# New order of a half in a gated convolution and state-space step: gates between the u tiles, convolution output kept in DRAM, phase tables from sines, planner durations reset

## The chip, the cores and the metric

The kernel runs on one core of one Trainium2 chip. The metric is device time in microseconds (us) of one execution. The kernel before takes 1961.19 us (median of three runs, 1960.9 to 1964.42).

## The reference, cut to what matters

One layer is applied to 2048 prompt tokens and to 8 single tokens that carry a state. Width 1024, state-space branch 512 wide in 32 groups of 16 channels with 64 complex states, convolution of 31 taps.

```
h    = rmsnorm(x, g_pre)
proj = h @ w_in          # c_a, c_b, c_z (1024 each), s_x, s_z (512 each), g_c, g_s (1024 each)
u    = c_a * sigmoid(c_b)
v    = silu(layernorm(causal_depthwise_conv(u))) * silu(c_z)
y_c  = v @ w_pc
ys   = gelu(ssm_branch(s_x))          # s_t = lambda * s_(t-1) + B u_t, lambda = exp((a_re + i a_im) dt)
ys   = ys * sigmoid(ys @ w_glu + b_glu) * silu(s_z)
y_s  = ys @ w_ps
o    = (sigmoid(g_c) * y_c + sigmoid(g_s) * y_s) @ w_out
x1   = x + rmsnorm(o, g_post)
e    = rmsnorm(p @ w_ple, g_ple)
y    = x1 + e * sigmoid(x1 @ w_pg + b_pg)
```

## The kernel before, in words

Channels lie on the 128 partitions, tokens along the free side. The tokens go in two halves: half 0 has 1024 prompt tokens and the 8 single ones (1032 columns in three blocks of 344), half 1 has 1024 (two blocks of 512). From `w_out` on, half 0 is worked in two parts of 516 columns, each as two blocks of 258. Every product is made in three fp32r matmuls: high part of the activations with high and low part of the weights, and low part with the high one (lines 289 to 291 of `stages`; lines 307 to 309 of `stage_pair`, where two weights share one pass). A name that ends in h or l is such a part: `hh`/`hl` of h, `yh`/`yl` of the gelu'd SSM output, `ynh`/`ynl` of the gated one, `mh`/`ml` first of the gate sum and then of x1.

A **stage** is one weight tile of 128 output channels: raw weights come by DMA on SP's queue into one of two buffers, ScalarE casts them to `whi` (line 252), GpSimd subtracts for `wlo` (line 332), one stage ahead of its use. TensorE runs the stage block by block into one of six PSUM banks, and a function given with the stage empties each bank. All engines run their instructions in the order in which the program emits them.

The order of emission comes from two sources. The list `order` (lines 218 to 234) gives the weight tiles: in half 0 the SX tiles (s_x) twice (first block, then the two others), CB and CA of each u tile, the eight GC gates, SZ, `w_glu`, then two GS gates ahead of each of the four `w_ps`, CZ, `w_pc`, `w_out`, `w_pg`. Half 1 is alike. Everything beside the stages is a task of a planner, `Background` (lines 30 to 104): a task is a generator that names an engine and a ready time, `use` adds an estimated duration (`cV`, `cS`, `cG`, lines 138 to 142) to that engine's clock, `pick` chooses VectorE or GpSimd, and `pump` emits all that should have begun by TensorE's estimated time. `drain` emits a task to its end at once, whatever the clocks say. Tasks are the norms (`mean_task`, `rstd_task`, `norm_task`), the convolution (`conv_task`: 31 multiply-adds on VectorE into an accumulator `acc` in PSUM, with some taps made by ScalarE and GpSimd, `cq` and `ca`), the state-space tables (`ssm_setup`, among them the phase tables `ph` by repeated doubling, and the transposes of `gt` by TensorE, line 610), the state-space batches (`ssm_batch`: scans between two turns by the phases), the layer norm, the x1 tiles (per tile a multiply `o<-o,prm,oacc` of line 183, an add `o<-o,xr`, a cast `mh<-o` on ScalarE, and `ml<-o,mh`) and the h tiles of the next half (`xn`, `hh`, `hl`). Activations of 128 x 1096 live in 38 SBUF units, taken and freed as the program goes; `room(n)` makes a task wait for n free ones.

Of the kernel before, what the change touches and what calls it, by code (L numbers as in the profile page):

```python
# [23 lines left out]
NUNIT = 38  # L24
UW = 1096


class Background:
# [19 lines left out]
    def pump(self, until=None, prio=1e9, only=None, pe=True):  # L48
        end = self.pe if until is None else until
        low = min(self.now, end)  # L50
        while True:
            best, first = None, 0.0
            for t in self.tasks:
                if t[0] > prio:
                    break
                e, r = t[1]
                if e == "P" and only and r > self.pe and not any(t is x for x in only):
                    continue
                if e == "P" and not pe:
                    continue  # L60
                at = max(self.clock[e], r) if e in self.clock else r + (1.2 if e == "P" else 0.0)
                if at <= end and (best is None or at < first - 0.05):
                    best, first = t, at
            if best is None:
                self.now = end
                return
            self.now = max(low, first)
            try:
                best[1] = next(best[2])
            except StopIteration:  # L70
                best[3] = True
                self.tasks.remove(best)
# [61 lines left out]
def build(nc, tc, A, O):  # L134
# [23 lines left out]
    with ExitStack() as ctx:  # L158
# [60 lines left out]
        for h in range(2):  # L219
            if h == 0:  # L220
                order += [("w_ple", j) for j in range(2)]
            for _ in range(2 if h == 0 else 1):
                order += [("w_in", SX + b) for b in range(4)]
            for c in range(8):
                order += [("w_in", CB + c), ("w_in", CA + c)]
# [56 lines left out]
        def stages(key, todo):  # L282
            wt, k = take(key)
            for i, (m, rhs, evac, c0, n) in enumerate(todo):
# [9 lines left out]
                bg.pe += 3 * k * (n / 2400.0 + 0.003)  # L294
# [3 lines left out]
        def stage_pair(keys, rhs, blocks, evacs):  # L298
# [12 lines left out]
            bg.pe += 6 * len(rhs) * sum(n / 2400.0 + 0.003 for _, n in blocks)  # L311
# [36 lines left out]
        def mean_task(acc, blocks, bias, ready, k, split):  # L348
# [11 lines left out]
            yield "P", ready  # L360
# [32 lines left out]
        def norm_task(acc, blocks, ready, split=False):  # L393

            c = slice(blocks[0][0], blocks[-1][0] + blocks[-1][1])
            (tmp, y), r = yield from mean_task(acc, blocks, epsc, ready, 2, split)
# [14 lines left out]
        ud_d = [dram.tile([P, HT + NS], F32, name=f"ud{b}") for b in range(NB)]  # L411
        yd_d = [dram.tile([P, 8, 136], F32, name=f"yd{b}") for b in range(NB)]
# [18 lines left out]
        MAGIC = 12582912.0  # L431

# [15 lines left out]
        tables = {"done": 0}  # L448

        def ssm_setup():  # L450
# [20 lines left out]
            r0 = use("V", 5.6, 3.0)  # L471
# [8 lines left out]
            r0 = use("V", 1.6, r0)  # L480
# [25 lines left out]
            r0 = use("V", 4.0, r0)  # L506
# [19 lines left out]
            r0 = use("V", 6.0, r0)  # L526
# [16 lines left out]

            yield "V", r0
            tt(k1, mag, mag)
            tt(k1, k1, k1)
            tt(rho, k1, k1)
            ph = [[k1, k2], [k3, nre]]

            def unit_length(re, im, t):  # L550

                tt(t[0], re, re)
                tt(t[1], im, im)
                tt(t[0], t[0], t[1], ALU.add)
                ts(t[0], t[0], -0.5, 1.5)
                tt(re, re, t[0])
                tt(im, im, t[0])

            v2 = [wk[:, x * 16:x * 16 + 16] for x in range(2)]
            V.tensor_copy(out=ph[0][0], in_=cs)  # L560
            V.tensor_copy(out=ph[0][1], in_=sn)
            for x in range(3):
                unit_length(*ph[0], v2)
                cmul(*ph[1], *ph[0], *ph[0], *v2)
                ph.reverse()
            r0 = use("V", 6.5, r0)
            for x in range(2):
                yield from room(3)
                pu2 = [alloc(name="ph") for _ in range(3)]
                un = [t[:, 0:1024].rearrange("p (j k) -> p j k", k=P) for t in pu2[0:2]]  # L570
                w2 = [pu2[2][:, y * 512:(y + 1) * 512].rearrange("p (j k) -> p j k", j=8) for y in range(2)]
                s2 = [t[:, 0:8] for t in v2]
                yield "V", r0
                for r in range(2):
                    V.tensor_copy(out=un[r][:, :, 0], in_=ph[0][r][:, x * 8:x * 8 + 8])
                m = 1
                while m < P:
                    unit_length(un[0][:, :, m - 1], un[1][:, :, m - 1], s2)
                    base = [u_[:, :, m - 1:m].to_broadcast([P, 8, m]) for u_ in un]
                    cmul(un[0][:, :, m:2 * m], un[1][:, :, m:2 * m], un[0][:, :, 0:m], un[1][:, :, 0:m],  # L580
                         *base, w2[0][:, :, 0:m], w2[1][:, :, 0:m])
                    m *= 2
                    r0 = use("V", 2.0 + 6 * cV(4 * m), r0)
                    yield "V", r0
                for b in range(2 * x, 2 * x + 2):
                    for r in range(2):
                        dma(out=ph_d[b][:, r * 512:(r + 1) * 512],
                            in_=pu2[r][:, (b - 2 * x) * 512:(b - 2 * x + 1) * 512], after=r0)
                free(*pu2)
            r1 = max(r0, r1)  # L590
            for b in range(NB):
# [11 lines left out]
                r1 = use("V", 6 * cV(512), r1)  # L603
                we = alloc(name="we")
                wev = we[:, 0:1024].rearrange("p (j i r s) -> p j i r s", i=2, r=2, s=64)
                for r in range(2):
                    yield "P", r1
# [7 lines left out]
                yield "P", r1  # L615
# [7 lines left out]
                free(gt)  # L623
                yield "V", r3
# [13 lines left out]
                free(kdu, we)  # L638
                cq = alloc(name="cq")
# [18 lines left out]
                tables[b] = queue["data"] + 1.0  # L658
            free(bb, bcu, cbd, pu)
# [16 lines left out]
        def ssm_batch(h, b, sx, ysb, n, ready):  # L676
# [25 lines left out]
            phu = alloc(name="sph")  # L702
            rp = dma(out=phu[:, 0:1024], in_=ph_d[b], after=tables[b])
# [8 lines left out]
            for j0 in range(0, 4, 2):  # L712
                yield "P", r
# [16 lines left out]
            r = max(r1, rp)  # L730
# [16 lines left out]
            r = use("V", 2 * cV(1024) + 2 * cV(512), r)  # L747
# [6 lines left out]
            r = use("V", 8 * cV(256), r)  # L754
# [3 lines left out]
            r = use("V", 2 * cV(1024) + 2 * cV(512) + 0.2, r)  # L758
# [9 lines left out]
            for j0 in range(0, 4, 2):  # L768
                yield "P", r
# [51 lines left out]
        def conv_task(h, us, vs, seen):  # L821
            for c in range(NT):
                while us[c] is None:
# [10 lines left out]
                use("V", 0.4)  # L834
# [10 lines left out]
                use("V", 1.33)  # L845
                while left["lo"] <= left["hi"]:
# [6 lines left out]
                    r = use("V", 1.33)  # L853
# [34 lines left out]
        def sample_conv_task(seen):  # L888

            w = lambda c, k: cw[:, c, k:k + 1]  # L890
            for c in range(NT):
# [12 lines left out]
                use("V", 1.0, r)  # L904
# [23 lines left out]
        def embed(wait):  # L928

            for j in range(2):  # L930
                def ev_of(h, j=j):
# [3 lines left out]
                    def ev(m, o, c0, nn):  # L935
# [3 lines left out]
                        if c0 == 344:  # L939
                            V.tensor_copy(out=ts_[m][:, c0:c0 + nn], in_=o)  # L940
                            fore("V", cV(nn) + 0.06)
# [24 lines left out]
        def rms_task(todo):  # L966

            for nm, h in todo:
# [25 lines left out]
                r = yield from norm_task(acc, BLOCKS[h], ra, True)  # L994
# [85 lines left out]
        def half(h, hT, finish):  # L1080
# [16 lines left out]
            for k, part in enumerate(PARTS[h] if h == 0 else [[0, 1]]):  # L1097
                if finish:
                    finish(k)
                def ev_of(b):  # L1100
# [21 lines left out]
            us, vs = [None] * NT, [None] * NT  # L1122
            seen = [0, 0]
            conv = bg.add(conv_task(h, us, vs, seen), 10)
            samp = bg.add(sample_conv_task(seen), 9) if h == 0 else None
            for c in range(NT):
                sg = unit("sg")
                stage(("w_in", CB + c), hT, blocks, act_to(sg, AF.Sigmoid))
                u = unit("u")

                def ev_a(m, o, c0, nn, sg=sg, u=u):
                    tt(u[:, PAD + c0:PAD + c0 + nn], o, sg[:, c0:c0 + nn])
                    fore("V", cV(nn) + 0.06)

                stage(("w_in", CA + c), hT, blocks, ev_a)
                free(sg)
                us[c] = (u, bg.clock["V"] + 0.3)
# [3 lines left out]

            for c in range(NT):
                gc = unit("gc")
                stage(("w_in", GC + c), hT, blocks, act_to(gc, AF.Sigmoid))
                dma(out=gc_d[h][c * P:(c + 1) * P, 0:n], in_=gc[:, 0:n], after=bg.clock["S"] + 0.3)
                free(gc)
# [5 lines left out]
            def gelu_task(b):  # L1152
                yield "S", ready[b]
                zs[b] = alloc(name="z")
# [52 lines left out]
            def ysn_task(b):  # L1207
                yield "S", ready[b]
                ysn[b] = hilo("yn")
# [9 lines left out]
            cz, vT = [None] * NT, [None] * NT  # L1219
            zr = [0.0] * NT  # L1220

            lnt = {}

            def ln_sub(c, mean, acc, r):
                yield "V", r
                v = vs[c][0][:, PAD:PAD + n]
                r = ew("V", v, v, mean[:, full], ALU.subtract, n, r)
                if c:
                    yield from room(1)
                q = alloc(name="sq") if c else acc  # L1230
                yield "S", r
                S.activation(out=q[:, full], in_=v, func=AF.Square)
# [354 lines left out]
```

## Time and profile before

| | |
|---|---|
| profiled execution | 1960.78 us, span 1959.0 us |
| runs | 1960.9, 1961.19, 1964.42 us |
| granted clock of TensorE, mean | 0.991 |
| busy: PE / DVE / ACT / POOL | 1915.9 / 1438.4 / 769.3 / 784.2 us |
| DMA | 243.63 MB, mean 124 GB/s |
| share of the chain that ended last: PE / DVE / issue / POOL / ACT | 84 / 4 / 3 / 2 / 2 % |

TensorE has work for 98% of the span. The page's slices show where it has not: the first two slices (0 to 98 us) and the fourth and fifth (147 to 245 us). The table of waits names what it waited for each time.

### The profile page before, as it was taken

How to read it: one execution, taken by the hardware profiler on the slowest of the kernel's cores; microseconds unless marked ns; L12 is line 12 of the kernel's file. 1: busy time of each engine (PE TensorE's matmuls, PEld its weight loads, DVE VectorE, ACT ScalarE, POOL GpSimd, SP SyncE). 2: the span in 40 equal slices, each digit the busy share in tenths (PEclk: the TensorE clock that was granted, in tenths of full speed). 3: DMA queues.
4: the chain of work that ended last, by engine and by line, in shares of the span. 5: the costliest groups of instructions: out<-in, count | busy, mean ns of one | idle time of the engine just before them, and what ended most of it. 6: DMA issues, size and time to landing. Idle time of an engine off the chain costs nothing.

```text
span 1959.0 us, 27432 instructions
## 1 busy us (share of the span) xinstructions
PE 1915.9 (98%) x10772; PEld 1723.5 (88%) x10772; DVE 1438.4 (73%) x1703; ACT 769.3 (39%) x1301; POOL 784.2 (40%) x573
## 2 busy tenths in 40 slices
PE   8897999999999999999999999999999999999998
PEld 7897999999999999999997888888788888888876
DVE  6889997899899876446674579888499843341786
ACT  7424211228311364255533223455731353223542
POOL 1437523315422233234452222786743223224554
PEclk9898999999999999999999999999999999999999
DMA  8461334542122215334564563222112311432455
GB/s 316 152 209 56 106 133 142 181 141 71 57 89 80 99 43 194 120 95 144 193 207 162 183 204 119 65 65 97 66 43 76 99 65 44 161 108 86 140 193 172
DMA packets 103290, 243.63 MB, mean 124 GB/s; under 512 B 11752, under 2 KB 41576, under 8 KB 103144
## 3 DMA queue, kind: packets, MB, share of 16 engines
q1 hardware_dynamic: 102840, 241.68, 37.0%
q8 instruction: 84, 1.38, 0.3%
q14 instruction: 46, 0.38, 0.1%
q10 hardware_dynamic: 320, 0.20, 0.0%
HBM read 188.17 MB, written 54.62 MB: 124 GB/s over the span
## 4 chain that ended last, share of the span: by engine, by line
PE 84%; DVE 4%; issue 3%; POOL 2%; ACT 2%; DMA 1%; SPq 0%; ACTq 0%; POOLq 0%; DVEq 0%
PE bank L289 27%; PE bank L291 26%; PE bank L290 26%; PE bank L775 2%; POOL ca L332 1%; PE bank L778 1%; PE bank L720 1%; DVE sgp L332 1%; POOL wlo L332 1%; DVE o L183 1%; DMA raw<-in_w 1%; DVE spar L183 0%; DVE o L332 0%; PE bank L620 0%; DMA xn<-in_xT 0%
## 5 line engine op out<-in xcount | busy, mean ns | idle before, releaser
L332 POOL TENSOR_TENSOR wlo<-raw,whi 128x512 fp32r<-128x512 f32 x386 | 565.7, 1484 | 1072.2 <-ACT whi L252 1056.8
L289 PE MATMUL bank<-hh,whi 128*128 128x344 f32 (+1 forms) x1888 | 666.1, 353 | 0.9 <-ACT whi L252 0.9
L290 PE MATMUL bank<-hl,whi 128*128 128x344 f32 (+1 forms) x1888 | 661.4, 350 | 5.3 <-DVE hl L332 5.3
L291 PE MATMUL bank<-hh,wlo 128*128 128x344 f32 (+1 forms) x1888 | 659.8, 349 | 1.5 <-POOL wlo L332 1.5
L183 DVE SCALAR_TENSOR_TENSOR acc<-u,prm,acc 128x1024 f32<-128x1024 f32 x412 | 530.5, 1288 | 11.2
L289 PEld LDWEIGHTS bank<-hh,whi 128*128 128x128 f32 x1888 | 356.6, 189 | 37.5 <-ACT whi L252 1.5
L290 PEld LDWEIGHTS bank<-hl,whi 128*128 128x128 f32 x1888 | 357.1, 189 | 36.8 <-DVE hl L332 5.6
L291 PEld LDWEIGHTS bank<-hh,wlo 128*128 128x128 f32 x1888 | 357.4, 189 | 34.7 <-POOL wlo L332 2.5
L252 ACT CAST whi<-raw 128x512 fp32r<-128x512 f32 x388 | 223.9, 619 | 144.0 <-PE bank L290 68.7
L289 PE MATMUL bank<-mh,whi 128*128 128x258 f32 (+1 forms) x768 | 247.0, 322 | 2.2 <-ACT mh L339 1.7
L291 PE MATMUL bank<-mh,wlo 128*128 128x258 f32 (+1 forms) x768 | 246.6, 321 | 1.7 <-POOL wlo L332 1.6
L290 PE MATMUL bank<-ml,whi 128*128 128x258 f32 (+1 forms) x768 | 246.5, 321 | 0.4 <-DVE ml L332 0.3
L291 PEld LDWEIGHTS bank<-mh,wlo 128*128 128x128 f32 x768 | 145.6, 190 | 14.3 <-POOL wlo L332 3.0
L289 PEld LDWEIGHTS bank<-mh,whi 128*128 128x128 f32 x768 | 145.4, 189 | 14.2 <-ACT mh L339 1.9
L290 PEld LDWEIGHTS bank<-ml,whi 128*128 128x128 f32 x768 | 145.5, 189 | 12.5 <-DVE ml L332 1.0
L332 POOL TENSOR_TENSOR ca<-ca,cq 128x512 f32<-128x512 f32 x104 | 132.3, 1300 | 38.9 <-ACT cq L882 35.6
L290 PE MATMUL bank<-vl,whi 128*128 128x344 f32 (+1 forms) x320 | 111.9, 350 | 0.7 <-DVE vl L332 0.7
L289 PE MATMUL bank<-vh,whi 128*128 128x344 f32 (+1 forms) x320 | 112.0, 350 | 0.0
L291 PE MATMUL bank<-vh,wlo 128*128 128x344 f32 (+1 forms) x320 | 111.9, 350 | 0.0
L882 ACT ACTIVATE cq<-u,prm 128x512 f32<-128x512 f32 x104 | 73.4, 722 | 55.1 <-POOL ca L332 46.0
L332 DVE TENSOR_TENSOR oacc<-oacc,sq 128x258 f32<-128x258 f32 (+1 forms) x42 | 29.7, 721 | 70.2 <-ACT sq L1389 69.9
L177 DVE TENSOR_TENSOR gcl<-bank,gcl 128x344 f32<-128x344 f32 (+1 forms) x40 | 23.5, 587 | 65.4 <-PE bank L291 65.3
(213 smaller groups left out, 2452.0 us busy)
## 6 DMA issues: line engine op xcount, KB each, us to landing
raw<-in_w SPq DMA_DIRECT2D x194, 512.0 KB
cq<-cq SPq DMA_DIRECT2D x12, 512.0 KB
e<-e SPq DMA_DIRECT2D x8, 516.0 KB
rt<-e SPq DMA_DIRECT2D x8, 516.0 KB
gc<-gc SPq DMA_DIRECT2D x8, 516.0 KB
m<-gs SPq DMA_DIRECT2D x8, 516.0 KB
gcl<-gc SPq DMA_DIRECT2D x8, 516.0 KB
m2l<-m SPq DMA_DIRECT2D x8, 516.0 KB
```

What stands on the lines that cost most here:

```text
L177: V.tensor_tensor(out=out, in0=a, in1=b, op=op)
L183: V.scalar_tensor_tensor(out=out, in0=a, scalar=s, in1=b, op0=op0, op1=op1)
L252: S.copy(out=hi, in_=t[:, c])
L289: T.matmul(o, hi[:, w], rh[:, c0:c0 + n], start=kt == 0, stop=False)
L290: T.matmul(o, hi[:, w], rl[:, c0:c0 + n], start=False, stop=False)
L291: T.matmul(o, lo[:, w], rh[:, c0:c0 + n], start=False, stop=kt == k - 1)
L332: (V if e == "V" else GP).tensor_tensor(out=out, in0=a, in1=b, op=op)
L720: T.matmul(pvs[rr][half_[i], jj], we[:, g * P + rr * 64:g * P + rr * 64 + 64], U[:, g, 8:8 + ne], start=True, stop=True)
L775: T.matmul(pvs[i][:, jj], TW[:, :, 2 * j + i], U[:, 2 * j + i, o0:136], start=True, stop=False)
L778: T.matmul(pvs[i][:, jj], cq[half_[i], x * 512 + j * P:x * 512 + (j + 1) * P], X[half_[i], x, j, o0:136], start=False, stop=x == 1)
L882: S.activation(out=q[:, h], in_=u[:, k + x * 512:k + x * 512 + 512], func=AF.Identity, scale=w(k))
```

## The change

1. Half 0 starts with two u tiles on block 0 (in place of SX), then the same two on blocks 1 and 2, then the four SX tiles, then the other u tiles. Two of the 16 gate stages follow each later u tile; the rest of the gates come ahead of SZ. In half 1 all eight u tiles have two gates each.
2. All gates, the GS ones too, are stored to DRAM. The GS gates are loaded again as `gs` before `w_ps`, and the four `w_ps` follow each other directly after `w_glu`.
3. The convolution's output tiles 0 to 5 may be stored to DRAM (`v_d`) and loaded again by `back_task`, added after `w_ps`.
4. The phase tables are made with Sin on ScalarE and products on GpSimd (`phases`), in place of doubling on VectorE.
5. The planner's durations are new, and a task's matmul may be marked "Q": it is laid 9 us of planned time later.

The transposes move to line 655, the helpers to lines 343, 184 and 190, and the products to lines 300 to 302 of the changed kernel. Core of the diff:

```
+                if e == "Q":
+                    e, r = "P", r + MARGIN
-        return "V" if v + n / 960.0 <= g + n / 478.0 + 0.3 else "G"
+        return "V" if v + n / 760.0 <= g + n / 440.0 + 0.4 else "G"
-    cV = lambda n: 0.08 + n / 960.0
+    cV = lambda n: 0.12 + n / 760.0
-    cS = lambda n: 0.13 + n / 1250.0
-    cG = lambda n: 0.16 + n / 478.0
+    cS = lambda n: 0.15 + n / 1100.0
+    cG = lambda n: 0.3 + n / 440.0
...
-            order += [("w_in", GC + c) for c in range(8)]
+            for c in range(0 if h else EARLY, 8):
+                order += [("w_in", CB + c), ("w_in", CA + c)] + gates[:2]
+                gates = gates[2:]
+            order += gates
             order += [("w_in", SZ + b) for b in range(4)]
             order += [("w_glu", j) for j in range(2)]
-            for j in range(4):
-                order += [("w_in", GS + 2 * j), ("w_in", GS + 2 * j + 1), ("w_ps", j)]
+            order += [("w_ps", j) for j in range(4)]
...
+            def phases(x, r):
...
+                r = ew("G", v3(a), kb, part(hi), ALU.mult, 1024, r)
+                r2 = ew("G", v3(cp), kb, part(lo), ALU.mult, 1024, r)
...
+                S.activation(out=sp, in_=a, func=AF.Sin, scale=PI)
+                S.activation(out=cp, in_=q, func=AF.Sin, scale=-PI, bias=hpi)
...
-            for x in range(2):
-                yield from room(3)
...
-                    unit_length(un[0][:, :, m - 1], un[1][:, :, m - 1], s2)
...
-                    cmul(un[0][:, :, m:2 * m], un[1][:, :, m:2 * m], un[0][:, :, 0:m], un[1][:, :, 0:m],
-                         *base, w2[0][:, :, 0:m], w2[1][:, :, 0:m])
...
+            def back_task():
+                lnt["back"] = True
+                for c in list(lnt["out"]):
+                    yield from room(6)
+                    t = alloc(name="v")
+                    vs[c] = t, dma(out=t[:, PAD:PAD + n], in_=v_d[h][c * P:(c + 1) * P, 0:n])
...
+            load_gs(0)
             for j in range(4):
-                gs = [unit("gs") for _ in range(2)]
-                for x in range(2):
-                    stage(("w_in", GS + 2 * j + x), hT, blocks, act_to(gs[x], AF.Sigmoid))
                 if j == 0:
                     bg.drain(*yt)
...
                 stt(o[:, cc], o[:, cc], vcol("g_post", c), acc[:, cc], ALU.mult, ALU.mult)
-                r = max(use("V", cV(m), r), rx)
+                r = max(use("V", 0.2 + m / 420.0, r), rx)
```

Three places show how instructions move. First, VectorE at the start, where it makes the low parts `hl` of the first half's blocks 1 and 2 (the 688 column rows). Before:

```order
L177 TENSOR_TENSOR acc_169<-acc_169,mean_339 128x688
...
L183 SCALAR_TENSOR_TENSOR xT_138<-xT_138,prm,acc_169 128x688
L183 SCALAR_TENSOR_TENSOR xT_139<-xT_139,prm,acc_169 128x688
...
L332 TENSOR_TENSOR hl_418<-xT_138,hh_417 128x688
L332 TENSOR_TENSOR hl_420<-xT_139,hh_419 128x688
```

The same place in the changed kernel, where `spar` are the 16 column parameters of the state-space branch and `u` is what empties a bank of a u tile:

```order
L184 TENSOR_TENSOR acc_173<-acc_173,mean_606 128x688
...
L184 TENSOR_TENSOR u_765<-bank,sg_687 128x344
L190 SCALAR_TENSOR_TENSOR xT_142<-xT_142,prm,acc_173 128x688
...
L190 SCALAR_TENSOR_TENSOR xT_144<-xT_144,prm,acc_173 128x688
L184 TENSOR_TENSOR u_839<-bank,sg_802 128x344
L343 TENSOR_TENSOR hl_416<-xT_142,hh_415 128x688
...
L190 SCALAR_TENSOR_TENSOR xT_147<-xT_147,prm,acc_173 128x688
...
L343 TENSOR_TENSOR hl_430<-xT_149,hh_429 128x688
```

The first `hl` tile now stands behind the emptying of the second u tile's block 0, and 14 rows of `spar`, left out here, stand ahead of it too, between the first row and the second.

Second, TensorE at the end of `w_glu` in half 0. Before, the products of `yh` are followed by two GS gates on `hh`, 144 matmuls, and only then by `ynh`:

```order
L290 MATMUL bank<-yl_4706,whi 128x344
L291 MATMUL bank<-yh_4705,wlo 128x344
L289 MATMUL bank<-hh_417,whi 128x344
L290 MATMUL bank<-hl_418,whi 128x344
...
L291 MATMUL bank<-hh_431,wlo 128x344
L289 MATMUL bank<-ynh_5183,whi 128x344
```

In the changed kernel:

```order
L300 MATMUL bank<-yh_5428,whi 128x344
L301 MATMUL bank<-yl_5429,whi 128x344
L302 MATMUL bank<-yh_5428,wlo 128x344
L300 MATMUL bank<-ynh_5914,whi 128x344
L301 MATMUL bank<-ynl_5915,whi 128x344
```

No stage is left between the two.

Third, ScalarE in part 1 of `w_out` of half 0, where `mh` are the high parts of part 0's x1 tiles and `whi` the weights of a coming stage. Before, the casts are spread over the stages:

```order
L339 CAST mh_7276<-o_8108 128x516
L339 CAST mh_7378<-o_8109 128x516
L321 COPY o_8110<-bank 128x258
L252 CAST whi<-raw 128x512 x2
...
L339 CAST mh_7489<-o_8110 128x516
...
L252 CAST whi<-raw 128x512 x2
...
L339 CAST mh_7597<-o_8111 128x516
...
L252 CAST whi<-raw 128x512 x2
```

In the changed kernel all eight stand within one stage:

```order
L263 CAST whi<-raw 128x512 x2
L350 CAST mh_7204<-o_8020 128x516
L350 CAST mh_7304<-o_8021 128x516
...
L350 CAST mh_7407<-o_8022 128x516
L350 CAST mh_7510<-o_8023 128x516
L350 CAST mh_7613<-o_8024 128x516
...
L350 CAST mh_7819<-o_8026 128x516
L350 CAST mh_7918<-o_8027 128x516
L332 COPY o_8023<-bank 128x258
L263 CAST whi<-raw 128x512 x2
```

The next cast of weights comes behind the last of them. The same lump stands in half 1.

## Rows read from the trace of the kernel before

**Rows 1.** The page, part 1: busy time of each engine, its share, instructions.

```profile
PE 1915.9 (98%) x10772; PEld 1723.5 (88%) x10772; DVE 1438.4 (73%) x1703; ACT 769.3 (39%) x1301; POOL 784.2 (40%) x573
```

**Rows 2.** TensorE's waits: what was waited for, total us, times, longest us.

```profile
PE bank L610 <- issue: 14.1, 1, 14.1
PE bank L289 <- ACT whi L252: 8.3, 3, 6.9
PE bank L290 <- DVE hl L332: 5.3, 1, 5.3
PE bank L289 <- ACT mh L339: 1.7, 1, 1.7
```

**Rows 3.** Stretches: bounds, length, busy of PE, PEld, DVE, ACT, POOL, clock, DMA.

```profile
522.40:545.00 22.60, 22.60 (x146) 22.60 (x145) 19.62 (x22) 8.61 (x14) 10.30 (x6) 1.00 0.18 53
890.00:936.00 46.00, 46.00 (x381) 45.89 (x380) 30.84 (x41) 26.38 (x60) 22.98 (x16) 1.00 0.45 149
84.50:88.00 3.50, 3.40 (x12) 3.40 (x13) 2.77 (x21) 1.73 (x4) 0.00 (x0) 0.50 0.05 20
196.00:200.00 4.00, 3.77 (x15) 3.80 (x16) 3.93 (x7) 1.21 (x2) 1.28 (x1) 0.50 0.39 137
990.00:994.00 4.00, 4.00 (x22) 4.00 (x23) 3.93 (x4) 1.79 (x5) 2.98 (x2) 0.59 0.17 63
```

**Rows 4.** Timeline, 186 to 198 us, VectorE and TensorE: start, us, instruction, idle before.

```profile
188.84 2.02 DVE L177 TENSOR_TENSOR ph<-ph 128x512 f32<-128x512 f32 x3
195.44 0.69 DVE L177 TENSOR_TENSOR gt<-gw 128x512 f32<-128x512 f32 x1
196.23 1.09 PE L610 MATMUL bank<-ident,gt 128*128 128x128 f32 x4 [14.06 <-issue]
```

**Rows 5.** Timeline, 50 to 85 us, VectorE and TensorE, and a group of VectorE's.

```profile
50.86 2.63 DVE L183 SCALAR_TENSOR_TENSOR xT<-xT,prm,acc 128x688 f32<-128x688 f32 x3
83.68 0.87 DVE L332 TENSOR_TENSOR hl<-xT,hh 128x688 fp32r<-128x688 f32 x1
84.60 0.65 PE L290 MATMUL bank<-hl,whi 128*128 128x344 f32 x1 [5.33 <-DVE hl L332]
L332 DVE TENSOR_TENSOR hl<-xT,hh 128x688 fp32r<-128x688 f32 x7 | 5.9, 871 | 4.0 <-ACT hh L339 4.0
```

**Rows 6.** Timeline of ScalarE and VectorE after `w_glu` of half 0.

```profile
522.63 0.55 ACT L1192 ACTIVATE sgl<-bank,prm 128x344 f32<-128x344 f32 x1 [1.36 <-PE bank L291]
523.08 3.91 ACT L339 CAST ynh<-z 128x1032 fp32r<-128x1032 f32 x4
524.16 4.67 DVE L332 TENSOR_TENSOR ynl<-z,ynh 128x1032 fp32r<-128x1032 f32 x4 [0.43 <-ACT ynh L339]
L332 DVE TENSOR_TENSOR ynl<-z,ynh 128x1024 fp32r<-128x1024 f32 x4 | 4.6, 1217 | 0.0
```

**Rows 7.** Timeline of VectorE, 901 to 964 us, and groups of x1 instructions.

```profile
901.32 0.69 DVE L177 TENSOR_TENSOR oacc<-oacc,mean 128x516 f32<-128x516 f32 x1
931.94 0.70 DVE L332 TENSOR_TENSOR ml<-o,mh 128x516 fp32r<-128x516 f32 x1 [0.35 <-ACT mh L339]
955.60 0.74 DVE L183 SCALAR_TENSOR_TENSOR o<-o,prm,oacc 128x516 f32<-128x516 f32 x1
962.83 3.48 DVE L183 SCALAR_TENSOR_TENSOR o<-o,prm,oacc 128x516 f32<-128x516 f32 x2
L183 DVE SCALAR_TENSOR_TENSOR o<-o,prm,oacc 128x516 f32<-128x516 f32 x16 | 21.9, 1396 | 0.0
L332 DVE TENSOR_TENSOR o<-o,xr 128x516 f32<-128x516 f32 x16 | 15.0, 959 | 0.0
L332 DVE TENSOR_TENSOR ml<-o,mh 128x516 fp32r<-128x516 f32 x16 | 11.8, 762 | 1.4 <-ACT mh L339 1.3
```

**Rows 8.** TensorE's waits from 1896 to 1920 us (`w_pg` of half 1).

```profile
PE bank L291 <- POOL wlo L332: 1.6, 2, 1.1
PE bank L289 <- ACT whi L252: 0.5, 1, 0.5
```

More of the change, by code (lines that the diff above doesn't have):

```diff
@@ L24 @@
 NUNIT = 38
+NSPILL = 6
+MARGIN = 9.0
+EARLY = 2
 UW = 1096
@@ L310, in stage_pair @@
             w_ahead(wstate["use"], 0)
-            bg.pe += 6 * len(rhs) * sum(n / 2400.0 + 0.003 for _, n in blocks)
+            bg.pe += 6 * len(rhs) * sum(cPr(n) for _, n in blocks)
             bg.pump(pe=False)
@@ L411, in build @@
         ud_d = [dram.tile([P, HT + NS], F32, name=f"ud{b}") for b in range(NB)]
+        v_d = [dram.tile([D, HT + NS], F32, name=f"v{h}") for h in range(2)]
         yd_d = [dram.tile([P, 8, 136], F32, name=f"yd{b}") for b in range(NB)]
@@ L446, in exp_dve @@
             tt(out, q, ki.bitcast(F32))
-        tables = {"done": 0}
+        tables = {"done": 0, "phases": 0}
         def ssm_setup():
@@ L507, in ssm_setup, with phase_task @@
+            def phase_task(r):
+                for x in range(2):
+                    yield from phases(x, r)
+            bg.add(phase_task(r0), 6.1)
             yield "V", r0
@@ L658, in ssm_setup @@
                 tables[b] = queue["data"] + 1.0
+            while tables["phases"] < NB:
+                yield None, bg.now + 0.5
             free(bb, bcu, cbd, pu)
@@ L729, in ssm_batch @@
             free(we)
-            r = max(r1, rp)
+            while tables["phases"] < b + 1:
+                yield None, bg.now + 1.0
+            yield from room(3)
+            phu = alloc(name="sph")
+            r = max(r1, dma(out=phu[:, 0:1024], in_=ph_d[b], after=tables["ph", b // 2]))
+            yield from room(2)
             tmp, tm2 = alloc(name="stmp"), alloc(name="stmq")
@@ L1099, in half @@
+            ln = bg.add(ln_task(), 4)
+            conv = bg.add(conv_task(h, us, vs, seen), 10)
+            samp = bg.add(sample_conv_task(seen), 9) if h == 0 else None
+            if h == 0:
+                for k, part in enumerate(PARTS[h]):
                     finish(k)
+                    for c in range(EARLY):
+                        u_tile(c, [blocks[i] for i in part])
+            for part in [list(range(len(blocks)))]:
                 def ev_of(b):
@@ L1121, in half, with gate @@
                 bg.add(rms_task([("e", 1)]), 7)
[L1122 to L1137, printed above, removed]
+            def gate(i):
+                t = unit("gc")
+                stage(("w_in", (GC, GS)[i // 8] + i % 8), hT, blocks, act_to(t, AF.Sigmoid))
+                dma(out=(gc_d, m2_d)[i // 8][h][i % 8 * P:(i % 8 + 1) * P, 0:n], in_=t[:, 0:n],
+                    after=bg.clock["S"] + 0.3)
+                free(t)
+            gate_at = 0
+            for c in range(0 if h else EARLY, NT):
+                u_tile(c, blocks)
+                for _ in range(2):
+                    gate(gate_at)
+                    gate_at += 1
             if h == 0:
                 dma(out=O["conv_old"], in_=A["cache"][:, 1:, :])
[L1142 to L1146, printed above, removed]
+            while gate_at < 16:
+                gate(gate_at)
+                gate_at += 1
             bg.drain(*tasks, wait=False)
```

358 lines of the change are left out of this document (215 added, 143 removed).

## The prediction

> **What bounds the kernel now.** I read the page first: TensorE is busy for 1915.9 of 1959.0 us, VectorE for 1438.4 [rows 1]. The change leaves TensorE's matmuls as they are, 10,120 rows of the program before and after. So less work elsewhere (VectorE 1705 instructions to 1488, GpSimd 578 to 655, ScalarE 1303 to 1380) gives nothing by itself, and the sum is one of TensorE's stalls: which go, which come. The second view is TensorE's waits [rows 2]. One is large, 14.1 us before the first transposes (L610). Of the 8.3 us for `whi`, 6.9 is the first weight load, which stays. Third come the stretches: 144 matmuls of 344 columns take 22.6 us, 0.157 us each, and between 890 and 936 us, where x1 is made beside `w_out`, TensorE never waits although VectorE is busy for 30.8 us of 46 [rows 3].
>
> The stretches show a second price. After the 5.3 us wait and after the 14.1 us one the granted clock is 0.50 [rows 3], which is 1.2 of 2.4 GHz, and it is 0.59 over the 4 us after the 1.7 us wait for `mh`. In the 3.5 us after the first, 12 matmuls are done where 3.5 / 0.157 = 22 would have been, so 10 x 0.157 = 1.6 us are lost, and the rise ends a few matmuls later. I count 1.7 us for every stall of some 2 us or more, added or removed.
>
> **The start.** Before, the 688 column `xT` begin right after the norm, at 50.86, and the last `hl`, behind the parameters, starts at 83.68; TensorE waits 5.33 us for it, until 84.60 [rows 5]. Four stages of block 0 are done by then, and 7/8 of the next one, 3.3 of 24 x 0.157 = 3.77 us, so block 0 ends at 84.6 - 5.3 - 3.5 = 75.8. In the changed order (two u tiles in place of the SX, the same four stages) all eight `hl` and five `xT` stand behind the eviction of the second u tile's block 0, which waits for that end. With 0.5 for the eviction, 8 x 0.87 and 5 x 0.88 (2.63 for three [rows 5]) the last `hl` ends at 87.7; TensorE needs it at 79.3. The wait is 8.4 in place of 5.3, and longer beside `wlo`. I take +4; the ends are -5 (it goes, GpSimd or gaps taking the rows) and +7. The clock fell there before, too.
>
> **What goes.** The transposes wait for `gt`. The timeline shows why: VectorE does the doubling (`ph`, still 2.02 us at 188.84) ahead of the `gt` products, and the transposes start 0.1 us behind the end of the first `gt`, 195.44 + 0.69 [rows 4]. In the changed kernel VectorE doubles nothing, and behind the last `hl` stand parameters, four evictions and seven taps, then `gt`: by the durations of such rows in the trace some 35 us, 40 with small operations at the slow 1.2 us that they have beside `wlo`, so about 123 to 128. TensorE has 14 more blocks of 3.77 us ahead of the transposes from 75.8 (eight of the u tiles, six of SX), and the stall: 75.8 + 8.4 + 1.7 + 52.8 = 139. I take the stall as gone: -14.1 - 1.7 = -15.8. The ends are that, and 0, where as much as before stands ahead of `gt`.
>
> At the second part's `w_pg` in half 0 the wait for `mh` was 1.7 us [rows 2]. The x1 rows now come with 25 us of VectorE rows up to the last `ml`, before with 34, as the gate products stand behind them: -1.7 - 1.7 = -3.4, between 0 and that.
>
> **`w_glu` to `w_ps`.** Two GS stages of 11.3 us covered the making of `yn` [rows 3]. They are gone, the stage behind `w_glu` reads `ynh` and `ynl` at once. `w_glu`'s last bank is read at 522.63, some 0.2 us after its end; four `ynh` casts run from 523.08 to 526.99 and the fourth `ynl` ends at 528.83 [rows 6], 6.4 us behind 522.4. A stage with four pairs needs the fourth low part after 3 x 0.47 + 0.16 = 1.6 us. The stall is 4.8 us, with the clock 6.5. In half 1 the casts and `ynl` have the same sizes (4.6 us for four `ynl` [rows 6]) and a stage of 512 columns needs the last after 2.3: 4.5, with the clock 6.2. Together +12.7. The lower bound is 6, if the first two pairs are made while `w_glu` still runs; the upper is 15, if VectorE has a tap of 1.3 us between.
>
> **x1 beside `w_out`.** Before, the tiles are spread: the first multiply follows `oacc` (which ends at 902.0) and the last `ml` ends at 932.6, 30 us and five stages of 5.8 us later, with weight casts between [rows 7]. In the changed order eight adds, eight casts `mh` and six of the eight multiplies are laid into one stage, because its eviction drains older tasks, and the next `whi` stands behind them on ScalarE. VectorE's rows behind `oacc` are 8 x (1.396 + 0.959 + 0.762) = 25 us by the means. The chain begins some 4 us before that stage, the last `mh` is out at about +20, and the `whi` behind it was due when TensorE has worked that stage and the one after, at 2 x 5.8 = 11.6: a stall of 9 us. But the same multiply takes 0.74 alone and 1.74 beside GpSimd's `wlo` [rows 7], and while `whi` is held no `wlo` runs. With 2.1 us per tile the chain is 17 us and the stall 1 to 2. I take 5 us in half 0 and, with 14.9 us of rows in one stage, 4 in half 1, each with the clock: 5 + 4 + 3.4 = +12.4. Ends 0 and 22.
>
> The Trainium skill ("SBUF — State Buffer", "SBUF: two separate sides") says that a VectorE operation with two SBUF inputs and a GpSimd operation that reads SBUF take a port pair by an exclusive lock, and that the loser waits for the whole instruction. The trace agrees for this multiply: 0.74 alone against 3.48 / 2 = 1.74 [rows 7]. By that rule the lump speeds up as soon as GpSimd has no weights to split, the two stalls fall to 1 to 2 us each, and the sum is about +8 (1969); by the means they are 9 each and it is about +25 (1986).
>
> **`w_pg` of half 1.** It waited 1.6 + 0.5 = 2.1 us for weights [rows 8]. In the changed order the norm comes two stages later and all x1 tiles in one stage, VectorE 15 us against 5.6 of TensorE. I take a stall of 5 and the clock, 6.7 - 2.1 = +4.6, between -2 and +9.
>
> **Rest.** The layer norm of half 1 is laid into three stages in place of eight (VectorE 37 us against 33 of TensorE), +1 (0 to 5). ScalarE has 31 us of rows in two stages of 23.5 us around SZ of half 0, and seven h tiles, before five, are left to the end of half 0: together +1 (0 to 8). The convolution taps, the phase work of GpSimd (eight products per two batches, 11.7 us of rows per 11.3 us stage at most) and some 29 MB more DMA lie beside TensorE; I cost them at nothing as long as VectorE and GpSimd do not fall behind by a stage. If they do, a bank is emptied late, and each late stage costs its lateness once.
>
> **Sum.** -15.8 - 3.4 + 4 + 12.7 + 12.4 + 4.6 + 1 + 1 = +16.5. The profiled execution took 1960.8 us, 0.4 below the median of the runs shown: 1977.3, against the median 1977.7. I say 1977.
>
> **Rivals.**
> Covered: VectorE, with 73 us less of rows, is ahead at each of the new places, the lumps run at the price without GpSimd and hide, and the `yn` are begun early. Then -15.8 - 3.4 + 0 + 6 + 0 - 2 + 0 + 0 = -15, 1946. For it speaks the span from 890 to 936 without a wait; against it, that the fourth `ynl` depends on the last bank of `w_glu`, whoever is ahead. 0.22.
> Balance: the lumps hide, the start and `w_ps` cost what they cost: -19.2 + 4 + 12.7 + 0 + 2 = -0.5, 1960. 0.12.
> The stall stays: `gt` is late all the same, since the parameters are more (nine small operations for the phases) and each takes 1.2 us beside GpSimd. Half of 15.8 stays, and the lumps cost 9 each in place of 5 and 4: 1977 + 8 + 9 = 1994. Against it speaks that nothing long stands ahead of `gt`. 0.14.
> My forecast, 1966 to 1988 by its own bounds, has 0.52. It ends slower, and the Covered case on the other side; the lump decides from the point where the last `mh` comes less than 11.6 us behind the stage's start.
>
> This kernel's measurement can tell 0.2% from no change, about 4 us. Faster: Covered and a bit of Balance, 0.24. Same: 0.10. Slower: the rest, 0.66. The range goes from 1944, just under Covered, to 1996, just over the third rival, and leaves about 0.15 out.
>
> **What would show it.** Right: the largest wait at the transposes is gone; TensorE waits for `hl` by 8 us or more near 78 us; waits for `ynl` of 4 to 5 us twice, each followed by a clock near 0.5; a wait for `whi` in the second part of `w_out`, in each half, after the last of eight `mh`. Wrong: no wait at `ynl`, or `w_out` without one, or a long wait in the convolution's stretch for a bank or for weights behind a held DMA.

## The result and the profile after

The changed kernel takes 2006.99 us (median of four runs, 2006.52 to 2009.29) against 1961.05 us: ratio 1.0233, 95% interval 1.0215 to 1.0251. It is slower by 46 us. The forecast was slower, 1977 us, with a range from 1944 to 1996: the sign is right, the size is not.

The page of the changed kernel, part 1, answers to [rows 1]; its matmuls are the same in number, VectorE is busy for 55 us less, ScalarE for 60 and GpSimd for 118 us more:

```profile
PE 1935.8 (97%) x10772; PEld 1732.0 (86%) x10772; DVE 1383.7 (69%) x1486; ACT 828.9 (41%) x1378; POOL 901.9 (45%) x650
```

TensorE's waits of the changed kernel (total us, times, longest), which answer to [rows 2]:

```profile
PE bank L300 <- ACT whi L263: 22.2, 5, 6.9
PE bank L300 <- ACT mh L350: 10.3, 2, 10.1
PE bank L302 <- POOL wlo L343: 7.2, 7, 3.6
PE bank L319 <- DVE hl L343: 4.0, 5, 1.4
PE bank L318 <- ACT hh L350: 3.6, 1, 3.6
PE bank L300 <- ACT ynh L350: 3.3, 2, 1.7
```

The transposes have left the table. In their place stand the weights (`whi`, `wlo`), the x1 tiles (`mh`), the h tiles of the next half (lines 318 and 319) and `yn`. To price the places I take, in both traces, the time between the starts of two following matmuls beyond its usual 0.122, 0.157 or 0.232 us (258, 344 and 512 columns) and add it up over a stretch. This holds the waits and the lowered clock behind them.

| place (us in the changed trace) | before | after | change | predicted |
|---|---|---|---|---|
| start, `hl` of blocks 1 and 2 (60 to 100) | 11.4 | 10.1 | -1.3 | +4 |
| transposes (180 to 200 before) | 17.1 | 1.1 | -16.0 | -15.8 |
| SZ of half 0 (560) | 0.7 | 6.9 | +6.2 | in Rest |
| `w_glu` to `w_ps`, both halves (600, 1560) | 0 | 11.1 | +11.1 | +12.7 |
| x1 beside `w_out`, both halves (914, 1872) | 0 | 19.9 | +19.9 | +12.4 |
| second `w_pg` of half 0 (971) | 4.3 | 5.5 | +1.2 | -3.4 |
| between the halves (1040 to 1072) | 5.7 | 11.6 | +5.9 | in Rest |
| taps of half 1 (1160 to 1320) | 15.9 | 21.5 | +5.6 | 0 |
| x1 and `w_pg` of half 1 (1910, 1946) | 3.3 | 16.9 | +13.6 | +4.6 |

They sum to +46.2; over the whole traces the excess goes from 88.8 to 135.2 us.

**The lump**, the eight casts `mh` and what makes them, laid into one stage. Timeline of the changed kernel from 901 to 924 us, all four engines (start, us, instruction, idle before):

```profile
901.53 1.41 DVE L190 SCALAR_TENSOR_TENSOR o<-o,prm,oacc 128x516 f32<-128x516 f32 x2
...
908.70 0.75 DVE L190 SCALAR_TENSOR_TENSOR o<-o,prm,oacc 128x516 f32<-128x516 f32 x1
...
919.66 0.62 ACT L350 CAST mh<-o 128x516 fp32r<-128x516 f32 x1 [1.37 <-DVE o L343]
920.20 0.37 ACT L332 COPY o<-bank 128x258 f32<-128x258 f32 x1
920.46 1.14 ACT L263 CAST whi<-raw 128x512 fp32r<-128x512 f32 x2
...
921.16 5.27 POOL L343 TENSOR_TENSOR wlo<-raw,whi 128x512 fp32r<-128x512 f32 x4 [14.15 <-ACT whi L263]
...
921.13 0.58 PE L300 MATMUL bank<-mh,whi 128*128 128x258 f32 x1 [6.77 <-ACT whi L263]
922.77 0.58 PE L302 MATMUL bank<-mh,wlo 128*128 128x258 f32 x1 [0.84 <-POOL wlo L343]
```

ScalarE sits on the casts, each waiting for VectorE, until 920.28; a bank that TensorE filled at about 908.6 is emptied at 920.20, and the weights come behind. GpSimd stands idle for 14.15 us. The multiply takes 0.75 us there, the price that it had without GpSimd [rows 7], and its mean over half 0 falls from 1396 ns to 936:

```profile
L190 DVE SCALAR_TENSOR_TENSOR o<-o,prm,oacc 128x516 f32<-128x516 f32 x16 | 14.7, 936 | 0.0
```

**The granted clock**, stretches of the changed kernel, columns as in [rows 3]:

```profile
921.00:925.00 4.00, 3.03 (x12) 2.73 (x13) 0.59 (x2) 2.19 (x6) 3.84 (x3) 0.50 0.10 6
1040.00:1072.00 32.00, 23.84 (x90) 17.23 (x90) 20.96 (x19) 9.77 (x12) 3.98 (x3) 0.95 0.45 163
1052.00:1056.00 4.00, 3.34 (x8) 2.69 (x9) 2.89 (x3) 1.04 (x1) 0.00 (x0) 0.60 0.89 345
1956.00:1960.00 4.00, 3.62 (x8) 2.63 (x9) 2.92 (x5) 0.94 (x2) 0.00 (x0) 0.50 0.21 66
```

After a long wait the clock is 0.50, 1.2 of 2.4 GHz, as before.

**`w_glu` to `w_ps`, SZ, the second `w_pg` of half 1.** Timeline of the changed kernel, TensorE, VectorE, ScalarE and GpSimd at these places:

```profile
602.71 3.90 ACT L350 CAST ynh<-z 128x1032 fp32r<-128x1032 f32 x4
603.78 4.66 DVE L343 TENSOR_TENSOR ynl<-z,ynh 128x1032 fp32r<-128x1032 f32 x4 [0.42 <-ACT ynh L350]
...
603.80 0.42 PE L300 MATMUL bank<-ynh,whi 128*128 128x344 f32 x1 [1.58 <-ACT ynh L350]
605.07 0.42 PE L301 MATMUL bank<-ynl,whi 128*128 128x344 f32 x1 [0.85 <-DVE ynl L343]
...
560.84 1.13 ACT L263 CAST whi<-raw 128x512 fp32r<-128x512 f32 x2
...
561.02 2.37 POOL L343 TENSOR_TENSOR z<-z,zt 128x1032 f32<-128x1032 f32 x1 [4.26 <-ACT zt L334]
563.35 3.48 POOL L343 TENSOR_TENSOR wlo<-raw,whi 128x512 fp32r<-128x512 f32 x2
...
565.65 0.66 PE L302 MATMUL bank<-hh,wlo 128*128 128x344 f32 x1 [3.57 <-POOL wlo L343]
...
1951.03 0.69 DVE L343 TENSOR_TENSOR o<-o,xr 128x512 f32<-128x512 f32 x1 [5.48 <-DMA xr<-in_xT]
...
1951.75 0.62 ACT L350 CAST mh<-o 128x512 fp32r<-128x512 f32 x1 [7.08 <-DVE o L343]
...
1956.38 0.80 PE L300 MATMUL bank<-mh,whi 128*128 128x512 f32 x1 [10.05 <-ACT mh L350]
```

The `yn` casts and their low parts take what [rows 6] had, and TensorE now meets them. At SZ, ScalarE is held by table loads and the norm of half 1's input, so the z product comes late on GpSimd and `wlo` stands behind it. In half 1 the last x1 tiles wait for a load of `xr`, 5.48 us, which no row of before showed.

**The taps of half 1.** VectorE and TensorE:

```profile
1177.15 0.68 DVE L184 TENSOR_TENSOR u<-bank,sg 128x512 f32<-128x512 f32 x1
1177.97 0.77 PE L300 MATMUL bank<-hh,whi 128*128 128x512 f32 x1 [3.43 <-ACT cq L934]
```

The view names a `cq` of ScalarE as what ended the wait. But that `cq` ends at 1177.96, 0.01 us ahead of the matmul, where the waits for one engine's result in this trace end 0.04 us ahead; and no cast of weights ran after 1171.69. The emptying of the `u` bank ends at 1177.83, 0.14 us ahead, as in the waits of e1 (13.2 us) and e8 (12.3 us) that the view does put down to `u`. So TensorE waited for a bank. VectorE came late to it: from 1156.96 it ran eight scans, one tap and two turns ahead of it.

### The profile page after: what moved, and what is told of

Read it like the earlier page. It is cut to its first block, busy times and chain, and to the rows that moved or that the text cites. A ratio compares the mean times of both kernels' runs of the same rounds, so it can differ in the third digit from the quotient of the medians.

```text
span 2005.4 us, 27460 instructions
## 1 busy us (share of the span) xinstructions
PE 1935.8 (97%) x10772; PEld 1732.0 (86%) x10772; DVE 1383.7 (69%) x1486; ACT 828.9 (41%) x1378; POOL 901.9 (45%) x650
## 2 busy tenths in 40 slices
DMA packets 111353, 273.10 MB, mean 136 GB/s; under 512 B 12648, under 2 KB 42472, under 8 KB 111208
## 4 chain that ended last, share of the span: by engine, by line
PE 83%; issue 5%; POOL 4%; ACT 2%; DVE 2%; DMA 0%; SPq 0%; POOLq 0%; ACTq 0%; DVEq 0%
PE bank L300 26%; PE bank L302 26%; PE bank L301 26%; POOL wlo L343 3%; PE bank L827 1%; POOL ca L343 1%; PE bank L830 1%; PE bank L767 1%; DVE hl L343 0%; PE bank L665 0%; ACT L334 0%; POOL yl L343 0%; ACT z L1332 0%; ACT L1332 0%; DVE xn L190 0%
## 5 line engine op out<-in xcount | busy, mean ns | idle before, releaser
L343 POOL TENSOR_TENSOR wlo<-raw,whi 128x512 fp32r<-128x512 f32 x386 | 557.7, 1463 | 949.0 <-ACT whi L263 939.8
L190 DVE SCALAR_TENSOR_TENSOR acc<-u,prm,acc 128x1024 f32<-128x1024 f32 x384 | 494.5, 1288 | 10.8
L343 POOL TENSOR_TENSOR ca<-ca,cq 128x512 f32<-128x512 f32 x160 | 224.4, 1428 | 55.6 <-ACT cq L934 55.3
L301 PEld LDWEIGHTS bank<-ml,whi 128*128 128x128 f32 x768 | 147.9, 193 | 12.7 <-DVE ml L343 1.1
L934 ACT ACTIVATE cq<-u,prm 128x512 f32<-128x512 f32 x160 | 112.1, 720 | 57.8 <-POOL ca L343 57.4
L334 ACT ACTIVATE gc<-bank 128x344 f32<-128x344 f32 (+1 forms) x80 | 41.0, 514 | 169.5 <-PE bank L302 169.5
```

The source lines that it names most:

```text
L190: V.scalar_tensor_tensor(out=out, in0=a, scalar=s, in1=b, op0=op0, op1=op1)
L301: T.matmul(o, hi[:, w], rl[:, c0:c0 + n], start=False, stop=False)
L334: S.activation(out=t[:, c0:c0 + n], in_=o, func=func)
L343: (V if e == "V" else GP).tensor_tensor(out=out, in0=a, in1=b, op=op)
L934: S.activation(out=q[:, h], in_=u[:, k + x * 512:k + x * 512 + 512], func=AF.Identity, scale=w(k))
```

## The experiments

All were timed against the kernel before on the same chip, three rounds, or five where said. The kernel before took 1959.4 us beside e1 to e4, 1961.7 beside e5 to e8 and 1961.4 beside e9 to e12, so a difference to the changed kernel, which was timed at another occasion beside 1961.05, can be some 2 us off.

**e1: the durations of before in the changed kernel.**

```diff
-    cV = lambda n: 0.12 + n / 760.0
+    cV = lambda n: 0.08 + n / 960.0
-    cS = lambda n: 0.15 + n / 1100.0
+    cS = lambda n: 0.13 + n / 1250.0
...
-                r = max(use("V", 0.2 + m / 420.0, r), rx)
+                r = max(use("V", cV(m), r), rx)
```

> The changed kernel with the planner's durations set back to those of before (cV, cS, cG, pick, the set-up, scan and x1 costs); order, spills, sine tables and the late matmuls stay. Theory A (the durations make the lumps: with them the planner's VectorE clock runs ahead and a drain emits eight x1 tiles at once): the eight casts mh are spread again as before, the waits for whi near 914 and 1872 us (19.9 us with the clock) and the wait for mh near 1946 (10.1 more than before) go, and the time falls from 2007 to about 1977. Theory B (the new order, the 29 MB more of DMA and GpSimd's 118 us more cause the loss, the durations only shift it): 2000 to 2010.

Measured: 1994.5 us, ratio 1.0176 (1.0161 to 1.0191). The casts `mh` are spread, no wait for `whi` is left in `w_out`, and the second `w_pg` of half 1 costs 3.3 us in place of 16.9. But two new waits of over 10 us come in the taps of half 1; TensorE's waits and VectorE's timeline of e1:

```profile
PE bank L827 <- DVE u L184: 15.3, 1, 15.3
PE bank L300 <- DVE u L184: 13.2, 1, 13.2
```

```profile
1158.53 9.23 DVE L190 SCALAR_TENSOR_TENSOR acc<-u,prm,acc 128x1024 f32<-128x1024 f32 x7
1167.66 0.68 DVE L184 TENSOR_TENSOR u<-bank,sg 128x512 f32<-128x512 f32 x1
```

The eviction of a u tile stands behind scans, turns and seven taps, which the short durations had laid ahead of it. So the durations are guilty of the lumps, but the old ones don't fit the new order either. Both theories miss the total.

**e2: the new durations alone, in the kernel before.** The same edit the other way, with the lines of the set-up, the scans and the taps.

> The kernel before with the new planner durations alone. Theory A: the lumps come into w_out and w_pg although order and DMA are as before; the stall at the transposes stays; 1961 + 20 + 10 = about 1991, at least 1980. Theory B: no lump that costs, 1957 to 1965.

Measured: 2056.7 us, ratio 1.0496 (1.0478 to 1.0513), 97 us slower, three times what theory A said. TensorE's waits of e2:

```profile
PE bank L291 <- ACT whi L254: 32.9, 5, 11.3
PE bank L291 <- ACT vh L341: 13.3, 4, 4.9
PE bank L612 <- DVE gt L179: 11.4, 1, 11.4
PE bank L291 <- ACT mh L341: 10.4, 2, 10.2
PE bank L780 <- DVE sc L179: 9.6, 1, 9.6
```

The lumps are there without the new order and without its DMA, which ends theory B. The waits for `vh` (layer norm into `w_pc`) and `sc` (scans) I had not foreseen. The one for `vh` comes again in e8, and in no other run: those two alone have the new durations together with the doubling. Why it comes was not tried.

**e3: two gate stages held back to stand between `w_glu` and `w_ps`.**

```diff
             gates = [("w_in", g + c) for g in (GC, GS) for c in range(8)]
+            held, gates = gates[14:], gates[:14]
...
             order += [("w_glu", j) for j in range(2)]
+            order += held
             order += [("w_ps", j) for j in range(4)]
```

> The changed kernel with the last two gate stages of each half laid between w_glu and w_ps. Theory A (the missing cover is the price of w_ps directly after w_glu): the waits for ynh and ynl near 602 and 1566 us go, 6.8 + 4.3 = 11 us with the clock, 1996. Theory B (what makes yn is late whatever stands ahead, or the stall moves to the weights of w_ps): 2003 to 2009.

Measured: 1993.2 us, ratio 1.0170 (1.0155 to 1.0185), 14 us under the changed kernel; theory A. The first matmul on `ynh` follows at full pace:

```profile
600.52 0.32 PE L302 MATMUL bank<-ynh,whi 128*128 128x344 f32 x1
```

The wait at SZ shrinks too, from 6.9 to 1.4 us, which I did not expect; the start of SZ comes two stages earlier there.

**e4: the squares ahead of the x1 tiles.**

```diff
-                        ot.append(bg.add(o_task(c, c0, nn, bg.clock["S"] + 0.2, sqs[c % 2]), 1))
+                        ot.append(bg.add(o_task(c, c0, nn, bg.clock["S"] + 0.2, sqs[c % 2]), -3))
```

> The changed kernel with one priority changed: the squares of w_out's tiles go ahead of the x1 tiles in the planner, so that the drain at an eviction emits squares alone; durations stay new. Theory A (the drain makes the lump, and ScalarE's in-order queue turns it into a stall of TensorE): at most three casts mh stand between two casts of weights, both waits for whi in w_out go (19.9 us), 1987 or a little less. Theory B (the x1 tiles are late because VectorE and the loads of xr are slow; spread, they are late for w_pg instead): 2000 to 2007, with the stall at the start of w_pg.

Measured: 1972.5 us, ratio 1.0066 (1.0050 to 1.0081), 34 us under the changed kernel, more than theory A said. ScalarE's timeline of e4 in the same stretch shows casts and weights in turn:

```profile
902.00 1.14 ACT L263 CAST whi<-raw 128x512 fp32r<-128x512 f32 x2
903.36 0.61 ACT L350 CAST mh<-o 128x516 fp32r<-128x516 f32 x1
907.74 1.15 ACT L263 CAST whi<-raw 128x512 fp32r<-128x512 f32 x2
```

By the same count as in the table, `w_out` goes from 19.9 to 2.8 us, the second `w_pg` of half 0 from 5.5 to 2.8, the stretch between the halves from 11.6 to 5.6, and x1 with `w_pg` in half 1 from 16.9 to 5.6. The lump's price is more than its own stall: what is late at `w_out` is late again at the places behind it.

**e5: the sine tables alone, in the kernel before (five rounds).** Edit: the function `phases` and its use, without the rest of the diff.

> The kernel before with the phase tables by sines alone; order, durations and gates as before. Theory A (VectorE's doubling ahead of gt is the 14.1 us stall): the transposes stand after 14 blocks of the first half's start in place of 30 and wait for little; the stall and its clock, 15.8 to 16.3 us, go and nothing else changes: 1959 to 1961 less 16, about 1944. Theory B (the u tiles laid ahead of SX remove it, not the tables): the stall is still there, or comes again where gt is now wanted earlier, 1955 to 1965. Theory C (eight products of 1024 columns per two batches on GpSimd hold up wlo and the taps): the stall goes, new waits for wlo or u come, 1950 to 1965.

Measured: 1971.5 us, ratio 1.0045 (1.0028 to 1.0062). The wait at the transposes goes, they run at 123.2 us without one. Theory C is nearest, though the time lies above its range and little of it is `wlo` (5.1 us in place of 3.1). TensorE's waits of e5:

```profile
PE bank L289 <- DVE u L177: 7.0, 2, 5.0
PE bank L815 <- DVE sc L177: 6.7, 3, 4.1
```

The scans start earlier, and the eviction of u tiles waits behind them (waits of 2.0 and 5.0 us, with the clock 10 us or more from 160 to 220); in half 1, where nothing of the tables is left to make, waits for the scans' products cost 9 us more. The edit also moves the load of the phase tables to a later point of each batch, in half 1 too, and no run separates that from the sines. In the old order the table change is a loss.

**e8: doubling back in the changed kernel.** Edit: the reverse of e5's.

> The changed kernel with the phase tables by doubling on VectorE again. Theory A (the tables decide over the stall, wherever the transposes stand): VectorE is behind by the doubling, some 73 us of rows, in the stretch where the taps fill it; a wait for gt, for an evicted bank of a u tile or for the scans comes, 10 us or more: 2017 or more. Theory B (the order of the start is what removes the stall): the same as the changed kernel, 2003 to 2010.

Measured: 2040.7 us, ratio 1.0396 (1.0376 to 1.0415), 34 us over the changed kernel, in the range of theory A. TensorE's waits and VectorE's timeline of e8:

```profile
PE bank L300 <- ACT vh L350: 14.4, 4, 6.0
PE bank L300 <- DVE u L184: 13.0, 2, 12.3
```

```profile
202.69 0.82 DVE L184 TENSOR_TENSOR ph<-ph 128x128 f32<-128x128 f32 x3
...
204.29 0.93 DVE L184 TENSOR_TENSOR u<-bank,sg 128x344 f32<-128x344 f32 x2
```

The long wait at about 192 is still VectorE's doubling, now through a bank of a u tile instead of the transposes. By the count of the table it costs 15 us, with the clock. That is less than half of the 34: the larger part, 26 us, lies in `w_pc` of half 0, where TensorE waits for the layer norm's `vh`, which theory A did not name, and the stall at SZ gives 6 us back.

**e6: e3 and e4 together (five rounds).**

> The changed kernel with both edits: two gates held back to w_ps, and the squares ahead of the x1 tiles. Theory A (the stalls are separate places and add): 2007 - 33 - 13 = 1961, within 4 us of the kernel before. Theory B (what is gained at one place is lost at the next, since the engines are only reached later): 1967 or more.

Measured: 1951.4 us, ratio 0.9945 (0.9929 to 0.9961): 10 us faster than the kernel before, some 55 than the changed one. The gains add, and more: 33 + 13 = 46 were expected. TensorE's waits of e6:

```profile
PE bank L302 <- ACT whi L265: 6.8, 1, 6.8
PE bank L302 <- ACT mh L352: 4.6, 2, 3.0
```

The largest that are left are the first weight load, the start of the second `w_pg` of half 1 and, in the taps of half 1, 3.7 us for the emptying of a `u` bank, as in the changed kernel.

**e7: e6 with the margin of late matmuls at 0.** Edit: `MARGIN = 0.0`.

> The kernel of e6 with the margin of late matmuls set to 0. Theory A (they only move inside TensorE's row; their operands are there long before): the same time within 4 us. Theory B (the margin is what keeps TensorE from waiting for the scans): new waits for sc, U or gt at the state-space matmuls, 5 to 20 us slower than e6.

Measured: 1965.8 us, ratio 1.0016 (1.0003 to 1.0029), 14 us over e6; theory B. Waits for the scans' products (4.2 us) and for the norms' parts come:

```profile
PE bank L832 <- DVE sc L184: 4.2, 4, 1.2
PE bank L378 <- DVE nl L345: 3.2, 3, 1.9
```

**e9: one duration of the changed kernel set back.**

```diff
-                r = max(use("V", 0.2 + m / 420.0, r), rx)
+                r = max(use("V", cV(m), r), rx)
```

> The changed kernel with one duration set back: the x1 multiply costs cV(m), 0.80 us for 516 columns, in place of 1.43. Theory A (this one number makes the lump): at most three casts mh stand between two casts of weights; the waits for whi in w_out go and with them those that follow from the late x1 (start of w_pg, h tiles of the next half), as with the squares first: 2007 - 30 = about 1975. Theory B (the lump is of all durations together): 1990 to 2007.

Measured: 1968.6 us, ratio 1.0043 (1.0027 to 1.0060), 38 us under the changed kernel; theory A. One number for one instruction holds most of the loss. The waits for `whi` behind the first load (7.1 us) are gone but for 0.4 us:

```profile
PE bank L300 <- ACT whi L263: 7.5, 2, 7.1
```

By the count of the table `w_out` costs nothing here, the stretch between the halves 2.0 us and x1 with `w_pg` in half 1 7.0; the second `w_pg` of half 0 stays, with 7.3.

**e10: that duration alone, in the kernel before.** The same line the other way.

> The kernel before with that one duration alone, 0.2 + m/420 for the x1 multiply. Theory A: eight casts mh in one stage of half 0 and seven in half 1, each a stall of 6 to 7 us with 3 of clock and weights behind it: 1960 + 18 = 1975 to 1990. Theory B: the old order leaves VectorE room to do the lump in time: 1957 to 1966.

Measured: 1993.1 us, ratio 1.0169 (1.0150 to 1.0187), 32 us slower, a little over theory A. TensorE's waits of e10:

```profile
PE bank L289 <- ACT whi L252: 18.6, 4, 6.3
PE bank L289 <- ACT mh L339: 12.8, 4, 5.0
```

**e11: e3 and e9 together; e12: e3, e4 and e9 together (five rounds each).**

> The changed kernel with two gates held back to w_ps and the x1 multiply's duration set back. Theory A: as the kernel of e6, 1947 to 1956, under the kernel before by about 0.5%. Theory B: the planner's clock without the true price lays x1 too early and VectorE's queue stands in the way of other evictions, 1960 or more.

> Both ways of spreading x1 (squares first and the old x1 duration) and the two held gates. Theory A: the lump is gone already by one of them, the second adds nothing: 1946 to 1955. Theory B: what waits are left for mh at the start of the second w_pg of half 1 (about 5 us with the clock) go too: 1942 to 1946.

Measured: 1955.9 us, ratio 0.9972 (0.9961 to 0.9982), and 1955.2 us, ratio 0.9968 (0.9955 to 0.9980). Both beat the kernel before. e11 lies at the upper end of its theory A; e12 misses both theories by 0.2 us and is no faster than e11, so the second way of spreading adds nothing. e6 has the lowest ratio, but its interval overlaps that of e12: which duration of the multiply is better with the squares first is not shown.

## Why the prediction was right or wrong

1. *Transposes.* Right in mechanism and size: -15.8 predicted, -16.0 measured. They run at 134.9 us without a wait, 14 us behind the end of the first `gt` (120.4); I had TensorE there at 139 and `gt` at 123 to 128. e8 and e5 show the limit of the reason: the tables had to leave VectorE, but alone, in the old order, that loses 10 us, with new waits for evictions and scans. That the stall had kept these apart is my reading, no run shows it.
2. *Start.* Wrong in sign, +4 predicted, -1.3 measured. The loss to `hl` did grow, by 2 us: TensorE waits in short pieces, 1.4 us at most, and loses 9.5 us with the clock between 72 and 90, where it lost 7.5 before. I put the end of block 0 at 75.8, as before, and the last `hl` at 87.7; they came at about 72.6 (the `u` eviction starts at 72.79) and 84.07, so both moved, and the lateness by little. What turns the sign is a term that I left out: before, two waits for weights at 65.8 and 67.2 us (0.9 and 0.8, with a granted clock of 0.82 to 0.83 from 65 to 75) cost 3.9 us, and in the changed kernel 0.5 is left of it.
3. *`w_glu` to `w_ps`.* Right: +12.7 predicted, +11.1 measured, and e3 takes it away with two stages of cover.
4. *x1 beside `w_out`.* Right mechanism, too small: 12.4 against 19.9. The chain took 18.8 us from the first multiply (901.53) to the end of the last `mh` (920.28), near the 17 without GpSimd: the multiply takes 1.79 us at 904.08, beside GpSimd's `wlo`, and 0.75 us once GpSimd is idle. The port pair rule of the Trainium skill ("SBUF — State Buffer", "SBUF: two separate sides") agrees with these two rows. The mis-sized part is the stall that I worked out from the 17 us, 1 to 2 us: it was 6.77 in half 0. Of the difference 2.8 us are the start, since I let the chain begin 4 us ahead of its stage and it began 1.2 ahead (901.5 against about 902.7); 1.8 are the chain's length, and 0.8 the emptying of a bank and the cast behind it. Then come `wlo` (0.84) and the clock, 10.0 in all where I had taken 6.7.
5. *The step that failed most: "Rest", and `w_pg` apart from the lump.* I priced x1's lateness once, at `w_out`, and gave `w_pg` of half 0 a gain of 3.4, half 1 a loss of 4.6 and the h tiles about nothing. Measured are +1.2, +13.6 and +5.9; with the 7.5 that `w_out` had too little they are 27 of the 29.7 us by which the sum was too small. e4 and e9, two different edits that both spread the tiles, show that 34 to 38 us hang on the lump as one cause. VectorE's waits for loads of `xr` go from 9.4 us to 0.5 and 0 there, and TensorE waits less for the norm of half 1 and for the h tiles. At the second `w_pg` of half 0 the two runs differ (2.8 and 7.3 us), so its share is open. I had read from the order that the lumps exist, and not asked which number of the change makes them. It is one duration, 0.2 + m/420 = 1.43 us, near the mean in the trace of before (1.396). By the code, the drain at an eviction then has to run the planner's VectorE clock far ahead, past all x1 tiles; e4, where the drain passes squares alone, bears that out. And the price does not hold in the order that it makes: planned at 1.43 the multiply takes 0.94 us in the changed kernel and 1.00 in e10, while planned at 0.80 it takes 1.39 in e9 (means of half 0).
6. *SZ and the taps of half 1.* +6.2 and +5.6 where I had 1 and 0. I had named ScalarE's 31 us of rows in two stages and still let TensorE hide it. In the taps TensorE waits 3.43 us up to 1177.97 for a `u` bank that VectorE empties late, behind scans and turns. I had left this at nothing "as long as VectorE and GpSimd do not fall behind by a stage"; VectorE did.

Chance and range: the range ended at 1996, just over my slowest rival. My own upper ends, taken together with the transposes gone, make +50, which is 2011; I set the range as if they would not come together, and with one cause behind the lump, `w_pg` and the h tiles they did. `w_pg` of both halves and Rest even passed their own ends.

Open: why the new durations cost 97 us in the old order (e2), of which the lump explains 32 (e10). By the count of the table the largest other places are `w_pc` of half 0 (25 us, waits for `vh`), the scans from 440 to 480 (19) and a cast of weights near 1482 (15); their causes were not tried. The 29 MB more of DMA: no wait of TensorE names a load, and e4 and e9 move the same 273.10 MB without the long wait for `xr`; a kernel without the spills was not tried.

## What to carry to other kernels

When a planner's costs change, compare what each engine's queue holds between two casts of weights before reading any cost: a duration read from a trace can order worse, since a forced drain emits everything that its clock passes, and in the order that it makes the instruction may take another time. Before a stage is moved away, ask what it covered; two stages put back were worth 14 us here. Price a late chain at every place that needs its results, not once.

## What the runs showed of the hardware

One wait of 10.05 us is followed by 4 us at a granted clock of 0.50 (1956 to 1960). Between the halves, seven waits of 0.4 to 3.6 us, 8.2 in all, left a mean of 0.95 over 32 us; the clock was low once, 0.60 from 1052 to 1056, behind the longest of them. At the start, waits of 1.4, 1.1 and 1.0 us that end at 74.3, 77.5 and 79.2 are followed by 0.50:

```profile
79.00:82.00 3.00, 2.66 (x8) 2.22 (x8) 3.00 (x5) 0.56 (x2) 0.00 (x0) 0.50 0.00 0
```

I had counted 1.7 us of clock for every wait of some 2 us or more; behind the lump it is 2.4 us (10.0 less 6.77 and 0.84), and 3.4 for the pieces between the halves (11.6 less 8.2).
